# Decoder layer with latent attention: scores over 128 rows, regrouped query columns, and each mixer product's first weights loaded one product early

## The chip, the cores and the metric

One program on one core of a Trainium2 chip. The metric is the device time of one execution, in microseconds (us); three executions of the kernel before were timed, and one execution of it was profiled.

## What is computed

One decoder layer over 256 positions of width 2048, in float32. A SwiGLU feed-forward with 5632 hidden columns, a token mixer, and a second feed-forward, each followed by a residual layer norm. The token mixer runs two groups of heads on the same normalised stream: eight heads of latent attention, and eight heads of a sparse attention with three branches. The latent attention is this part:

```python
q = (rms_norm(c_q, q_norm_g) @ w_uq).reshape(b, s, MLA_HEADS, MLA_NOPE_DIM + MLA_ROPE_DIM)   # 512 -> 8 x (128 + 64)
q_nope, q_rope = q[..., :128], rope(q[..., 128:], pos)
kv = (rms_norm(c_kv, kv_norm_g) @ w_ukv).reshape(b, s, MLA_HEADS, 128 + 128)                 # 256 -> 8 x (k_nope, v)
k_r = rope(k_rope, pos)                                                                      # 64 wide, one for all heads
sc = (einsum("bhqd,bhkd->bhqk", qn, k_nope) + einsum("bhqd,bkd->bhqk", qr, k_r)) * scale     # causal, per block of 128 queries
o = einsum("bhqk,bhkd->bhqd", softmax(where(mask, sc, NEG_INF)), v)
```

c_q (512 wide), c_kv (256), k_rope (64), the sparse attention's projections and its gates are columns of one product of the stream with w_in.

## The kernel before

**Weight products.** Each product with a weight is done in three TensorE passes (`mm3`, L84 to L88): a float32 operand is split into a high part and the rest, high by high, high by low and low by high are added up in one PSUM bank, and all three run as 512-column matmuls of the fp32r type. The activations (`thi`, `tlo`) are the stationary operand, 128 x 128; the weights (`whi`, `wlo`) move, up to 512 columns. `load` (L133) brings 256 rows of one chunk of weight columns (512 KB for 512 columns) by one DMA of SP's queue into a buffer `raw` or `sum`; ACT casts it to `whi` (L81), and DVE subtracts to get `wlo` (L82). `whi` and `wlo` have six buffers each, `raw` and `sum` five and three.

`gemm` (L169) runs one chunk of columns over all of its rows, for the two tiles t of 128 positions: at each piece of 256 rows `load`, 6 matmuls for t = 0, 6 for t = 1, then two ticks. At the last piece `finish(0, ...)` is called between the two sixes and `finish(1, ...)` after them.

**Order of the work.** PE and SP carry out their instructions in the order in which the code issues them. Side work (transposes of results, scores, softmax, products with the values) is written as generators which `spawn` puts into lanes; `tick` counts and lets each lane issue its next step when it is due. A result's transposes come `DTR = 7` ticks after its `finish`. On ACT and DVE a scheduler orders the instructions, outside the program's text.

**The mixer.** The main sequence stands at L623 to L648 and L965 to L983: w_in chunk 0 (`fin_a`, c_q), `w_in_b` (`fin_b`, c_kv, rotated key, gates), w_in chunk 3 (`fin_c`), then for head group 0 `mla_proj(0)`, `mla_att(0)`, w_in chunks 4 and 1, `mla_proj(1)`, `mla_att(1)`, w_in chunks 5 and 2, and the output projection, with the sparse attention's side work between them.

`mla_proj(g)` (L703) does four heads by four products: two chunks of w_uq with 384 columns (two heads of 128 + 64), two of w_ukv with 512 columns. `fin_q` (L707) copies the 128-wide parts, rotates the 64-wide parts on DVE, and transposes each head's two parts apart: a 128-wide one (L718) and a 64-wide one (L719), 8 transposes for one chunk and both tiles. The rotated query parts and the rotated key `krT` (L589, L617) lie on 64 partitions.

`mla_att(g)` (L754) has three units: the second tile of queries for heads 0 and 1, then for heads 2 and 3, and the first tile for all four. For each head and each block of 128 keys there are two plain f32 matmuls into the same place, one over 128 rows and one over 64:

```python
o = ps[:, h * K + b * P:h * K + (b + 1) * P]
PE.matmul(o, qnT[t][:, hh, :], knT[b][:, hh, :], start=True, stop=False)   # L764, 128 rows
PE.matmul(o, qrT[t][:, hh, :], krT[:, b, :], start=False, stop=True)       # L765, 64 rows
```

That makes 8 instructions in each unit, 48 in the kernel. In the functions below, the line numbers are those of the profile.

Of the kernel before, what the change touches and what calls it, by code (L numbers as in the profile page):

```python
# [18 lines left out]
P = 128  # L19
D = 2048  # L20
# [24 lines left out]
def layer(ctx: ExitStack, tc: tile.TileContext, a: dict, out: bass.AP):  # L45
# [86 lines left out]

    def load(w, c, pc, spare=False):  # L133

        ap, pairs, n = w[:3]
# [33 lines left out]
    def gemm(x, w, c, ks, finish, head=0, tail=0, spare=0, first=KT, each=None):  # L169
# [419 lines left out]
    krT = att.tile([RD, NT, P], F32, name="krT")  # L589
# [12 lines left out]
    def fin_b(t, ps):  # L602
        def go():
            o = rms(ps[:, :KVR], KVR)
            kr = work.tile([P, 1, RD], F32, name="kr")
            rope(kr, ps[:, KVR:KVR + RD].rearrange("p (h d) -> p h d", h=1), cst["cos64"][:, t, :],
                 cst["sin64"][:, t, :], 1, RD)
            z = stat.tile([P, 24], F32, name="gz")
# [8 lines left out]
            PE.transpose(pt[:RD, 0, :], kr[:, 0, :], ident)  # L617
            A.copy(krT[:, t, :], pt[:RD, 0, :])
# [4 lines left out]
    gemm(xin, w_in, 0, KALL, fin_a, head=HEAD, spare=SPARE)  # L623
    gemm(xin, W["w_in_b"], 0, KALL, fin_b)
# [23 lines left out]
    gemm(xin, w_in, 3, KALL, fin_c)  # L648
# [51 lines left out]
    def units(t):  # L700
        return [(0, 4)] if t == 0 else [(0, 2), (2, 2)]

    def mla_proj(g):  # L703
        qnT, qrT, knT, vm = ([am() for _ in range(NT)] for _ in range(4))
        qrT = [q[:RD] for q in qrT]

        def fin_q(hp):  # L707
            def fin(t, ps):
                def go():
                    pv = ps.rearrange("p (h d) -> p h d", h=2)  # L710
                    qt = wk([P, 3, HD])
                    A.copy(qt[:, 0:2, :], pv[:, :, 0:HD])
                    rope(qt[:, 2, :].rearrange("p (h d) -> p h d", h=2), pv[:, :, HD:], cst["cos64"][:, t, :],
                         cst["sin64"][:, t, :], 2, RD)
                    yield DTR
                    pt = new_bank().rearrange("p (a b) -> p a b", a=4)
                    for j in range(2):
                        PE.transpose(pt[:, j, :], qt[:, j, :], ident)  # L718
                        PE.transpose(pt[:RD, 2 + j, :], qt[:, 2, j * RD:(j + 1) * RD], ident)  # L719
                    A.copy(qnT[t][:, 2 * hp:2 * hp + 2, :], pt[:, 0:2, :])  # L720
                    A.copy(qrT[t][:, 2 * hp:2 * hp + 2, :], pt[:RD, 2:4, :])
                    flag("mq", g, hp, t)

                spawn(go(), f"mla{g}q{hp}{t}")
                steps()
            return fin

        def fin_kv(hp):
            def fin(t, ps):
                def go():  # L730
# [8 lines left out]
                    A.copy(knT[t][:, 2 * hp:2 * hp + 2, :], pt[:, 0:2, :])  # L739
# [5 lines left out]

        for hp in range(2):
            h0 = 4 * g + 2 * hp
            gemm(lambda k, t: sl(cq[t], k), W["mla_w_uq"], h0 // 2, list(range(4)), fin_q(hp))
        for hp in range(2):
            h0 = 4 * g + 2 * hp  # L750
            gemm(lambda k, t: sl(ckv[t], k), W["mla_w_ukv"], h0 // 2, list(range(2)), fin_kv(hp))
        return g, qnT, qrT, knT, vm

    def mla_att(g, qnT, qrT, knT, vm):  # L754
        def unit(t, h0, nh):
            K = (t + 1) * P
            for hp in range(h0 // 2, (h0 + nh) // 2):
                yield from until(("mq", g, hp, t), *[("mk", g, hp, b) for b in range(t + 1)])
# [47 lines left out]
    def q_proj(g):  # L806
# [15 lines left out]
        gemm(xin, w_in, 1 + g, KALL, fin)  # L822
# [5 lines left out]
    def compress(src, n):  # L828
# [28 lines left out]
        hid = att.tile([P, 2, 32], F32, name="hid", bufs=2)  # L857
# [107 lines left out]
    mla_att(*mla_proj(0))  # L965
# [3 lines left out]
    gemm(xin, w_in, 4, KALL, fin_kv2("sel"), each=lambda i: ln_res("ln1", i // 2) if i % 2 else None)  # L969
    q_proj(0)  # L970
    mla_att(*mla_proj(1))
    new_kv("win")
    gemm(xin, w_in, 5, KALL, fin_kv2("win"))
    nsa_att(0)
    q_proj(1)
# [37 lines left out]
_CHUNKS = {"w_in": (D, NCH), "w_in_b": (D, 344), "mla_w_uq": (QR, 384), "mla_w_ukv": (KVR, NCH), "w_out": (D, NCH)}  # L1013
# [58 lines left out]
```

## Time and profile before

| | us |
|---|---|
| three timed runs | 1799.69, 1799.92, 1803.29 |
| their median | 1799.92 |
| the profiled execution, its own time | 1798.44 |
| its span, first to last instruction | 1796.7 |
| PE's matmul records, busy | 1772.0 |
| DVE, busy | 1500.6 |
| ACT, busy | 967.7 |
| the mixer's stretch of the span, about | 700 to 1070 |

How to read it: the profile shows for each engine when an instruction ran and, for a gap, what ended it. A matmul's record lasts longer than its turn on the engine (the next begins before it ends), so PE's busy time says only that PE was seldom empty; what a matmul costs is the time from its start to the next one's start. An f32 matmul is carried out in two passes and has two records; an fp32r one has one.

### The profile page before, as it was taken

Reading aid. Unit: us, or ns where it says so; the run is one execution under the profiler, and the core shown is the slowest. Engines: PE = TensorE matmul, PEld = TensorE weight load, DVE = VectorE, ACT = ScalarE, POOL = GpSimd, SP = SyncE. Lnnn points to the kernel's source line nnn. Section 1 sums busy time; section 2 is a strip of 40 time slices with the busy share of each in tenths; the row PEclk is TensorE's granted clock in tenths of the full one; section 3 lists DMA queues with packets and bytes.
Section 4 is the critical chain, followed back from the end, with each engine's and each line's share of the span. In section 5 each row is a group of like instructions: output and inputs, shape, how many; then the busy total and the mean of one; then the engine's idle time right before and its main releaser. Section 6 shows DMA issues by size and latency. Waiting matters only on the chain. (4 is left out here: it accounts for less than half of the span.)

```text
span 1796.7 us, 22556 instructions
## 1 busy us (share of the span) xinstructions
PE 1772.0 (99%) x8194; PEld 1453.9 (81%) x8194; DVE 1500.6 (84%) x1987; ACT 967.7 (54%) x1277; POOL 17.5 (1%) x40
## 2 busy tenths in 40 slices
PE   8999999999999999999999999999999999999997
PEld 6888888888888888887788787878888888888886
DVE  7899799999699976766566687899899999799976
ACT  6556455565456555644455555556456565456541
POOL 0000000000000000000000000000000000000000
PEclk9999999999999999999999999999999999999999
DMA  9656555557356575556733353567556557456673
GB/s 316 229 203 213 178 194 188 194 204 252 133 199 213 196 252 174 169 175 204 272 127 129 118 175 135 194 188 245 176 190 209 200 196 241 147 201 208 206 244 105
DMA packets 120736, 350.02 MB, mean 195 GB/s; under 512 B 11168, under 2 KB 17584, under 8 KB 120624
## 3 DMA queue, kind: packets, MB, share of 16 engines
q1 hardware_dynamic: 119312, 344.37, 56.0%
q0 software_dynamic: 1312, 4.21, 0.9%
q8 instruction: 64, 1.05, 0.2%
q14 instruction: 48, 0.39, 0.1%
HBM read 346.44 MB, written 2.10 MB: 194 GB/s over the span
## 5 line engine op out<-in xcount | busy, mean ns | idle before, releaser
L86 PE MATMUL bank<-whi,thi 128*128 128x512 f32 (+2 forms) x2046 | 805.5, 394 | 3.9 <-ACT whi L81 2.2
L87 PE MATMUL bank<-wlo,thi 128*128 128x512 f32 (+2 forms) x2046 | 793.7, 388 | 2.8 <-DVE wlo L82 2.8
L88 PE MATMUL bank<-whi,tlo 128*128 128x512 f32 (+2 forms) x2046 | 793.9, 388 | 0.2
L81 ACT CAST whi<-raw 128x1024 fp32r<-128x1024 f32 (+2 forms) x533 | 510.4, 975 | 409.2 <-PE bank L88 312.0
L82 DVE TENSOR_TENSOR wlo<-raw,whi 128x1024 fp32r<-128x1024 f32 (+2 forms) x533 | 590.0, 1123 | 101.8 <-ACT whi L81 99.3
L86 PEld LDWEIGHTS bank<-whi,thi 128*128 128x128 f32 x2046 | 384.3, 188 | 86.7 <-issue 5.4
L88 PEld LDWEIGHTS bank<-whi,tlo 128*128 128x128 f32 x2046 | 384.1, 188 | 80.3 <-DVE tlo L82 1.9
L87 PEld LDWEIGHTS bank<-wlo,thi 128*128 128x128 f32 x2046 | 384.6, 188 | 78.6 <-DVE wlo L82 5.0
L81 ACT CAST whi<-sum 128x1024 fp32r<-128x1024 f32 x265 | 274.6, 1047 | 288.4 <-PE bank L88 166.1
L82 DVE TENSOR_TENSOR wlo<-sum,whi 128x1024 fp32r<-128x1024 f32 x265 | 316.1, 1212 | 72.0 <-ACT whi L81 71.8
L243 DVE TENSOR_TENSOR sum<-raw 128x1024 f32<-128x1024 f32 x88 | 107.3, 1219 | 38.1 <-DMA raw<-in_ffn_w_gate 18.6
L87 PE MATMUL bank<-wlo,m 128*128 128x512 f32 x352 | 137.4, 390 | 0.2
L88 PE MATMUL bank<-whi,m 128*128 128x512 f32 x352 | 137.0, 389 | 0.0
L86 PE MATMUL bank<-whi,m 128*128 128x512 f32 x352 | 136.9, 389 | 0.0
L87 PEld LDWEIGHTS bank<-wlo,m 128*128 128x128 f32 x352 | 66.1, 188 | 15.2 <-DVE wlo L82 1.7
L86 PEld LDWEIGHTS bank<-whi,m 128*128 128x128 f32 x352 | 66.1, 188 | 13.9
L88 PEld LDWEIGHTS bank<-whi,m 128*128 128x128 f32 x352 | 66.1, 188 | 13.5
L275 DVE TENSOR_TENSOR w<-bank,w 128x512 f32<-128x512 f32 x96 | 62.6, 681 | 0.0
L245 DVE TENSOR_TENSOR sum<-sum,raw 128x512 f32<-128x512 f32 x88 | 60.2, 684 | 0.7
L244 DVE TENSOR_TENSOR sum<-sum,raw 128x512 f32<-128x512 f32 x88 | 60.1, 683 | 0.3
L82 DVE TENSOR_TENSOR tlo<-bank,thi 128x512 fp32r<-128x512 f32 (+1 forms) x56 | 35.8, 645 | 5.0 <-ACT thi L81 4.7
L660 ACT ACTIVATE w<-w,mx 128x256 f32<-128x256 f32 (+1 forms) x48 | 21.3, 446 | 29.2 <-DVE mx L656 29.2
(187 smaller groups left out, 890.2 us busy)
## 6 DMA issues: line engine op xcount, KB each, us to landing
raw<-in_ffn_w_up SPq DMA_DIRECT2D x160, 512.0 KB, 4.7
raw<-in_ffn_w_gate SPq DMA_DIRECT2D x148, 512.0 KB, 4.9
raw<-in_ffn_w_down SPq DMA_DIRECT2D x134, 512.0 KB, 4.7
sum<-in_ffn_w_down SPq DMA_DIRECT2D x42, 512.0 KB, 7.0
raw<-in_ffn_gu SPq DMA_DIRECT2D x32, 512.0 KB, 4.8
raw<-in_w_in SPq DMA_DIRECT2D x30, 512.0 KB, 4.7
raw<-in_w_out SPq DMA_DIRECT2D x20, 512.0 KB, 3.2
sum<-in_w_in SPq DMA_DIRECT2D x18, 512.0 KB, 6.7
```

The source lines that it names most:

```text
L81: A.copy(hi, src)
L82: V.tensor_tensor(lo, src, f(hi), op=OP.subtract)
L86: PE.matmul(ps, xh, wh, start=first, stop=False)
L87: PE.matmul(ps, xh, wl, start=False, stop=False)
L88: PE.matmul(ps, xl, wh, start=False, stop=last)
L243: V.tensor_tensor(t13, a_, b_[:, 1:2, :].broadcast_to([P, 2, NCH]), op=OP.add)
L244: V.tensor_tensor(t24[:, 0], t13[:, 0], a_[:, 1], op=OP.add)
L245: V.tensor_tensor(t24[:, 1], t24[:, 0], b_[:, 0], op=OP.add)
L275: V.tensor_tensor(r, B[b], r, op=OP.add)
L660: A.activation(s[:, h, :], s[:, h, :], AF.Exp, bias=mx[:, h:h + 1], accum_out=sm[:, h:h + 1])
```

## The change

1. The host regroups w_uq's columns: first the 128-wide parts of all eight heads, then the 64-wide parts of all eight; three chunks of 512 columns in place of four of 384. A new product of w_uq's third chunk gives all rotated query parts at once (`fin_qr`), ahead of `mla_proj(0)`; `mla_proj(g)` has one product of w_uq (four heads).
2. The rotated query parts are transposed by pairs of heads, 128 rows each. The rotated key is written twice into a zeroed tile, into the upper and the lower 64 of 128 columns, and transposed twice, so that `krT[:, j]` has the key on the rows of head j of a pair and zeros on the other 64.
3. A score matmul takes all keys of the unit at once: 256 columns for the second tile of queries, 128 for the first. `knT` is kept by pairs of heads with both key blocks side by side.
4. `gemm` gets `nxt`: before `finish(0, ...)` it loads (and splits) the first piece of the product that comes next, and that product takes it from `ahead`. All products from w_in chunk 0 to the last q_proj have it.
5. `hid` in `compress` has one buffer in place of two.

```diff
+    ahead = {}
     def load(w, c, pc, spare=False):
+        if (id(w), c, pc[0]) in ahead:
+            return ahead.pop((id(w), c, pc[0]))
...
             if end:
+                if nxt:
+                    ahead[id(nxt[0]), nxt[1], nxt[2]] = load(nxt[0], nxt[1], [nxt[2] + j for j in range(KT)])
                 finish(0, ps[0])
...
-    krT = att.tile([RD, NT, P], F32, name="krT")
+    krT = att.tile([P, 2, NT, P], F32, name="krT")
...
-            kr = work.tile([P, 1, RD], F32, name="kr")
-            rope(kr, ps[:, KVR:KVR + RD]...)
+            kr = wk([P, 2, P])
+            V.memset(kr, 0.0)
+            rope(kr[:, 0:1, :RD], ps[:, KVR:KVR + RD]...)
+            V.tensor_copy(kr[:, 1, RD:], kr[:, 0, :RD])
...
-            PE.transpose(pt[:RD, 0, :], kr[:, 0, :], ident)
-            A.copy(krT[:, t, :], pt[:RD, 0, :])
+            for j in range(2):
+                PE.transpose(pt[:, j, :], kr[:, j, :], ident)
+            A.copy(krT[:, :, t, :], pt[:, 0:2, :])
...
+    def fin_qr(t, ps):
+        def go():
+            qt = wk([P, NCH])
+            qv = qt.rearrange("p (h d) -> p h d", d=RD)
+            rope(qv, ps.rearrange("p (h d) -> p h d", d=RD), cst["cos64"][:, t, :], cst["sin64"][:, t, :], 8, RD)
+            yield DTR
+            pt = new_bank().rearrange("p (a b) -> p a b", a=4)
+            for j in range(4):
+                PE.transpose(pt[:, j, :], qt[:, j * P:(j + 1) * P], ident)
+            A.copy(qrT[t], pt)
+            flag("mr", t)
...
+        gemm(lambda k, t: sl(cq[t], k), uq, g, list(range(4)), fin_q, nxt=(ukv, 2 * g, 0))
         for hp in range(2):
-            gemm(lambda k, t: sl(cq[t], k), W["mla_w_uq"], h0 // 2, list(range(4)), fin_q(hp))
-        for hp in range(2):
-            gemm(lambda k, t: sl(ckv[t], k), W["mla_w_ukv"], h0 // 2, list(range(2)), fin_kv(hp))
+            gemm(lambda k, t: sl(ckv[t], k), ukv, 2 * g + hp, list(range(2)), fin_kv(hp),
+                 nxt=nxt if hp else (ukv, 2 * g + 1, 0))
...
-                for b in range(t + 1):
-                    o = ps[:, h * K + b * P:h * K + (b + 1) * P]
-                    PE.matmul(o, qnT[t][:, hh, :], knT[b][:, hh, :], start=True, stop=False)
-                    PE.matmul(o, qrT[t][:, hh, :], krT[:, b, :], start=False, stop=True)
+                o = ps[:, h * K:(h + 1) * K]
+                PE.matmul(o, qnT[t][:, hh, :], knT[hh // 2][:, hh % 2]...[:, :K], start=True, stop=False)
+                PE.matmul(o, qrT[t][:, 2 * g + hh // 2, :], krT[:, hh % 2]...[:, :K], start=False, stop=True)
...
-    mla_att(*mla_proj(0))
+    gemm(lambda k, t: sl(cq[t], k), uq, 2, list(range(4)), fin_qr, nxt=(uq, 0, 0))
+    mla_att(*mla_proj(0, (w_in, 4, 0)))
```

The order of the instructions at three places. In the rows, a number behind a name is a buffer's; x4 says that four equal instructions follow each other.

PE, the first unit of scores of head group 0, before (the last row is work of the compressed branch that follows):

```order
L764 MATMUL bank_7112<-m_6813,m_6810 128x128
L765 MATMUL bank_7112<-krT_6157,m_6812 128x128
L764 MATMUL bank_7112<-m_6814,m_6810 128x128
L765 MATMUL bank_7112<-krT_6157,m_6812 128x128
L764 MATMUL bank_7112<-m_6813,m_6810 128x128
L765 MATMUL bank_7112<-krT_6157,m_6812 128x128
L764 MATMUL bank_7112<-m_6814,m_6810 128x128
L765 MATMUL bank_7112<-krT_6157,m_6812 128x128
L847 MATMUL bank_7071<-raw_7133,w_7037 32x256 x4
```

Four pairs, each a 128-row and a 64-row operand. Now, the same unit:

```order
L783 MATMUL bank_7102<-m_6875,m_6874 128x256
L785 MATMUL bank_7102<-krT_6157,m_6822 128x256
L783 MATMUL bank_7102<-m_6875,m_6874 128x256
L785 MATMUL bank_7102<-krT_6157,m_6822 128x256
L868 MATMUL bank_7061<-raw_7119,w_7027 32x256 x4
L86 MATMUL bank_7001<-whi_7127,thi_6110 128x512
```

Eight instructions that changed between a 128-row and a 64-row operand became four; `krT` has taken part as a 128-row operand in each second one.

ACT, head group 1: L720 and L721 copy the transposed queries out of PSUM (after PE's transposes into bank_7854 and bank_7861), L81 casts weights. Before, PE's next matmul behind those transposes is the first that reads whi_7870:

```order
L852 COPY w_7850<-bank_7557 128x256
L720 COPY m_7600<-bank_7854 128x256
L721 COPY m_7602<-bank_7854 64x256
L720 COPY m_7601<-bank_7861 128x256
L721 COPY m_7603<-bank_7861 64x256
L81 CAST whi_7870<-raw_7868 128x1024
L81 CAST whi_7896<-raw_7894 128x1024
```

The cast of whi_7870 stands behind the copies of both banks. Now, where L743 copies the transposed queries (bank_7748, bank_7754), and PE's next matmul behind those transposes is the first that reads whi_7762:

```order
L81 CAST whi_7762<-sum_7760 128x1024
L837 COPY m_7685<-bank_7680 128x512
L837 COPY m_7692<-bank_7687 128x512
L754 COPY w_7708<-bank_7694 128x256
L755 COPY m_7592<-bank_7694 128x256
L81 CAST whi_7794<-sum_7792 128x1024
L754 COPY w_7717<-bank_7695 128x256
L755 COPY m_7593<-bank_7695 128x256
L743 COPY m_7588<-bank_7748 128x512
L743 COPY m_7589<-bank_7754 128x512
L81 CAST whi_7841<-raw_7839 128x1024
```

The cast that PE reads next stands eight rows ahead of the copies of the transposed queries; whi_7794, for the piece after it, stands ahead of them too.

DVE, second tile of `fin_b`: the rotation ends (L575 before, L582 now) and the transposed latent is scaled (L480 before, L487 now). Before:

```order
L575 TENSOR_TENSOR kr_6608<-kr_6608,w_6609 128x64
L82 TENSOR_TENSOR wlo_6760<-raw_6757,whi_6759 128x1024
L611 TENSOR_SCALAR gz_6614<-gz_6614 128x24
L612 RECIPROCAL gates_6158<-gz_6614 128x24
L82 TENSOR_TENSOR wlo_6778<-raw_6775,whi_6777 128x1024
L480 TENSOR_SCALAR w_6682<-bank_6679,pack_356 128x128 x2
L480 TENSOR_SCALAR w_6695<-bank_6692,pack_356 128x128 x2
```

Two splits of weights stand between the rotation and the scaling. Now:

```order
L582 TENSOR_TENSOR w_6616<-w_6616,w_6618 128x64
L487 TENSOR_SCALAR w_6686<-bank_6683,pack_356 128x128
L617 COPY w_6616<-w_6616 128x64
L487 TENSOR_SCALAR w_6686<-bank_6683,pack_356 128x128
L621 TENSOR_SCALAR gz_6624<-gz_6624 128x24
```

The copy of the key's second half (L617 of the changed kernel, w_6616) stands behind the first scaling of bank_6683. PE's transposes there now (L482 the latent, L628 the key):

```order
L482 MATMUL bank_6683<-ident_87,w_6585 128x128 x2
L628 MATMUL bank_6691<-ident_87,w_6587 128x128 x2
L482 MATMUL bank_6697<-ident_87,w_6614 128x128 x2
L628 MATMUL bank_6705<-ident_87,w_6616 128x128 x2
L86 MATMUL bank_6631<-whi_6711,thi_6110 128x512
```

The second of the transposes into bank_6705 reads what that copy writes, and the scaling ahead of the copy waits for PE's transposes into bank_6683, four to six places ahead of it.

## Rows read from the trace of the kernel before

**Rows 1.** The page of the profile: its first line, the busy time of each engine (us, share of the span, instructions), and the granted TensorE clock in 40 slices of the span, in tenths of full speed.
```profile
span 1796.7 us, 22556 instructions
...
PE 1772.0 (99%) x8194; PEld 1453.9 (81%) x8194; DVE 1500.6 (84%) x1987; ACT 967.7 (54%) x1277; POOL 17.5 (1%) x40
...
PEclk9999999999999999999999999999999999999999
```

**Rows 2.** The waits of PE from 700 to 1100 us, the stretch that holds the token mixer: instruction that waited <- what ended the wait: us in total, times, longest. The list is complete.
```profile
PE bank L86 <- ACT thi L81: 2.5, 3, 1.7
PE bank L86 <- ACT whi L81: 1.8, 1, 1.8
PE bank L87 <- DVE wlo L82: 0.8, 1, 0.8
PE bank L88 <- DVE tlo L82: 0.7, 2, 0.4
```

**Rows 3.** Groups of PE instructions with shapes kept apart: the two lines of the latent attention's scores. An f32 matmul leaves two records, one for each of its passes, so x48 is 24 instructions. Busy time in us and mean ns of one record.
```profile
L764 PE MATMUL bank<-m 128*128 128x128 f32 x48 | 11.1, 313 | 0.0
L765 PE MATMUL bank<-krT,m 64*128 64x128 f32 x48 | 11.6, 322 | 0.0
```

**Rows 4.** Timeline of PE, one unit of scores (second tile of queries, one pair of heads: 8 instructions, 16 records): start us, duration us, line, out<-in, partitions x columns, records. Durations overlap, so a price is read from one start to the next. The last row is the work that follows the unit.
```profile
810.90 0.38 PE L764 MATMUL bank<-m 128*128 128x128 f32 x2
811.21 0.49 PE L765 MATMUL bank<-krT,m 64*128 64x128 f32 x2
...
813.71 0.49 PE L765 MATMUL bank<-krT,m 64*128 64x128 f32 x2
814.12 0.64 PE L847 MATMUL bank<-raw,w 128*32 128x256 f32 x8
```

**Rows 5.** Timeline of PE at f32 products of other lines, same columns: values by probabilities in full rows (821.52), scores of the sparse attention with 256 columns in full rows (961.63), and a product over 15 rows (949.22), each with the row that follows it.
```profile
821.52 1.05 PE L770 MATMUL bank<-w,m 128*128 128x128 f32 x8
822.40 0.39 PE L764 MATMUL bank<-m 128*128 128x128 f32 x2
...
949.22 0.69 PE L918 MATMUL bank<-w,vcmp 15*128 15x256 f32 x2
949.84 1.13 PE L921 MATMUL bank<-w,m 128*128 128x256 f32 x4
...
961.63 1.03 PE L911 MATMUL bank<-m 128*128 128x256 f32 x4
962.50 1.03 PE L921 MATMUL bank<-w,m 128*128 128x256 f32 x4
```

**Rows 6.** Timeline of PE in the query projection: the first and the eighth matmul of a run of eight with 384 columns, the first and the twelfth of a run of twelve with 512 columns, and the first and the last of a block of eight transposes with the second matmul behind it.
```profile
782.73 0.33 PE L87 MATMUL bank<-wlo,thi 128*128 128x384 f32 x1
...
783.94 0.34 PE L88 MATMUL bank<-whi,tlo 128*128 128x384 f32 x1
...
787.11 0.39 PE L86 MATMUL bank<-whi,thi 128*128 128x512 f32 x1
...
789.64 0.39 PE L88 MATMUL bank<-whi,tlo 128*128 128x512 f32 x1
...
796.21 0.27 PE L718 MATMUL bank<-ident,w 128*128 128x128 f32 x1
...
796.97 0.27 PE L719 MATMUL bank<-ident,w 128*64 128x128 f32 x1
...
797.31 0.39 PE L87 MATMUL bank<-wlo,thi 128*128 128x512 f32 x1
```

**Rows 7.** Timeline of PE at the second block of query transposes of the second head group; in brackets the idle time before a row, and what ended it.
```profile
884.56 0.27 PE L718 MATMUL bank<-ident,w 128*128 128x128 f32 x1
...
887.36 0.50 PE L86 MATMUL bank<-whi,thi 128*128 128x512 f32 x1 [1.77 <-ACT whi L81]
888.62 0.50 PE L87 MATMUL bank<-wlo,thi 128*128 128x512 f32 x1 [0.76 <-DVE wlo L82]
888.96 0.40 PE L88 MATMUL bank<-whi,tlo 128*128 128x512 f32 x1
```

**Rows 8.** Timeline of ACT over the same time.
```profile
881.89 0.37 ACT L852 COPY w<-bank 128x256 f32<-128x256 f32 x1
885.19 0.37 ACT L720 COPY m<-bank 128x256 f32<-128x256 f32 x1 [2.93 <-PE bank L719]
...
886.25 3.90 ACT L81 CAST whi<-raw 128x1024 fp32r<-128x1024 f32 x4
```

**Rows 9.** Timelines of PE and of DVE where the transposes of the normalised latent and of the rotated key stand.
```profile
763.56 0.38 PE L475 MATMUL bank<-ident,w 128*128 128x128 f32 x2
...
764.10 0.27 PE L617 MATMUL bank<-ident,kr 128*64 128x128 f32 x1
...
761.15 0.22 DVE L575 TENSOR_TENSOR kr<-kr,w 128x64 f32<-128x64 f32 x1
...
763.98 1.12 DVE L480 TENSOR_SCALAR w<-bank,pack 128x128 f32<-128x128 f32 x4
```

**Rows 10.** Groups with shapes kept apart: the two halves of a weight's split into a high and a low part, on ACT and on DVE.
```profile
L82 DVE TENSOR_TENSOR wlo<-raw,whi 128x1024 fp32r<-128x1024 f32 x433 | 520.6, 1218 | 86.5 <-ACT whi L81 84.0 <-DMA raw<-in_ln_b 1.5
L81 ACT CAST whi<-raw 128x1024 fp32r<-128x1024 f32 x433 | 448.9, 1053 | 300.6 <-PE bank L88 227.9 <-DMA raw<-in_ffn_w_gate 18.9 <-issue 15.5
```

More of the change, by code (lines that the diff above doesn't have):

```diff
@@ L167, in new_bank, with gemm @@
         return bank.tile([P, NCH], F32, name="bank")
-    def gemm(x, w, c, ks, finish, head=0, tail=0, spare=0, first=KT, each=None):
+    def gemm(x, w, c, ks, finish, head=0, tail=0, spare=0, first=KT, each=None, nxt=None):
         n = w[2]
@@ L698, in layer @@
     NSC = float(HD ** -0.5)
[L700 to L726, printed above, removed]
@@ new lines, in layer @@
+    qrT = []
+    def fin_qr(t, ps):
[9 more added lines that the diff above has]
+            flag("mr", t)
+        spawn(go(), f"mlar{t}")
+        steps()
@@ new lines, in mla_proj, with fin_q, go @@
+    def mla_proj(g, nxt):
+        qnT, knT, vm = ([am() for _ in range(2)] for _ in range(3))
+        knT = [k.rearrange("p (h t) q -> p h t q", h=2) for k in knT]
+        def fin_q(t, ps):
+            def go():
+                qt = wk([P, 4, HD])
+                A.copy(qt, ps.rearrange("p (h d) -> p h d", h=4))
+                yield DTR
+                pt = new_bank().rearrange("p (a b) -> p a b", a=4)
+                for j in range(4):
+                    PE.transpose(pt[:, j, :], qt[:, j, :], ident)
+                A.copy(qnT[t], pt)
+                flag("mq", g, t)
+            spawn(go(), f"mla{g}q{t}")
+            steps()
@@ L744, in fin_kv, with mla_att @@
             return fin
+        gemm(lambda k, t: sl(cq[t], k), uq, g, list(range(4)), fin_q, nxt=(ukv, 2 * g, 0))
         for hp in range(2):
[L747 to L754 removed]
+            gemm(lambda k, t: sl(ckv[t], k), ukv, 2 * g + hp, list(range(2)), fin_kv(hp),
+                 nxt=nxt if hp else (ukv, 2 * g + 1, 0))
+        return g, qnT, knT, vm
+    def mla_att(g, qnT, knT, vm):
         def unit(t, h0, nh):
             K = (t + 1) * P
+            yield from until(("mr", t), ("mq", g, t))
             for hp in range(h0 // 2, (h0 + nh) // 2):
[L758 removed]
+                yield from until(*[("mk", g, hp, b) for b in range(t + 1)])
             ps = new_bank()
@@ L761, in unit @@
                 hh = h0 + h
-                for b in range(t + 1):
-                    o = ps[:, h * K + b * P:h * K + (b + 1) * P]
-                    PE.matmul(o, qnT[t][:, hh, :], knT[b][:, hh, :], start=True, stop=False)
-                    PE.matmul(o, qrT[t][:, hh, :], krT[:, b, :], start=False, stop=True)
+                o = ps[:, h * K:(h + 1) * K]
+                PE.matmul(o, qnT[t][:, hh, :], knT[hh // 2][:, hh % 2].rearrange("p t q -> p (t q)")[:, :K], start=True,
+                          stop=False)
+                PE.matmul(o, qrT[t][:, 2 * g + hh // 2, :], krT[:, hh % 2].rearrange("p t q -> p (t q)")[:, :K],
+                          start=False, stop=True)
             pT = yield from causal(ps[:, :nh * K], t, nh, MSC, None)
@@ L804, in layer, with q_proj @@
     qTs = {}
-    def q_proj(g):
+    def q_proj(g, nxt):
         def fin(t, ps):
@@ L856, in compress @@
             PE.transpose(pt[:, m, :], hs[:, m * P:(m + 1) * P], ident)
-        hid = att.tile([P, 2, 32], F32, name="hid", bufs=2)
+        hid = att.tile([P, 2, 32], F32, name="hid", bufs=1)
         x = stat.tile([P, 2, 32], F32, name="gx", bufs=2)
@@ L963, in out_last @@
             steps()
-    mla_att(*mla_proj(0))
+    qrT += [am() for _ in range(NT)]
+    gemm(lambda k, t: sl(cq[t], k), uq, 2, list(range(4)), fin_qr, nxt=(uq, 0, 0))
+    mla_att(*mla_proj(0, (w_in, 4, 0)))
     spawn(compress(kcT, "k"), "C")
@@ L968, in layer @@
     new_kv("sel")
-    gemm(xin, w_in, 4, KALL, fin_kv2("sel"), each=lambda i: ln_res("ln1", i // 2) if i % 2 else None)
-    q_proj(0)
-    mla_att(*mla_proj(1))
+    gemm(xin, w_in, 4, KALL, fin_kv2("sel"), each=lambda i: ln_res("ln1", i // 2) if i % 2 else None,
+         nxt=(w_in, 1, 0))
+    q_proj(0, (uq, 1, 0))
+    mla_att(*mla_proj(1, (w_in, 5, 0)))
     new_kv("win")
-    gemm(xin, w_in, 5, KALL, fin_kv2("win"))
+    gemm(xin, w_in, 5, KALL, fin_kv2("win"), nxt=(w_in, 2, 0))
     nsa_att(0)
-    q_proj(1)
+    q_proj(1, (W["w_out"], 0, 0))
     nsa_att(1)
```

17 lines of the change are left out of this document (10 added, 7 removed).

## The prediction

> **What bounds the kernel now.** I read the page first. PE is busy for 1772.0 of 1796.7 us, DVE for 1500.6, and the granted clock stands at its upper level, 2.4 GHz, in all 40 slices [rows 1]. So the time is the sum of PE's turns, and a change counts as far as it shortens that sum or removes a wait of PE; time saved on ACT, DVE or the queues is worth nothing by itself. The waits of PE come next: over the stretch that holds the mixer there are 2.5 + 1.8 + 0.8 + 0.7 = 5.8 us [rows 2]. That list sets the limit for the early loads: they can give back only a wait that PE has. Two of its four rows (thi, tlo) wait for activations behind a layer norm, which no early weight touches. The other two, 1.8 us for whi and 0.8 us for wlo, are one place, looked at below. Last I read the timeline of PE for what each kind of matmul costs from start to start, because the records overlap.
>
> **The scores.** A unit takes from 810.90 to 814.12, 3.22 us for 8 instructions, or 0.40 us each [rows 4]. There are 24 instructions on each of the two lines [rows 3], six units, together 6 x 3.22 = 19.3 us. This is dear for what it does: the product of the values, as wide and as many columns but in full rows only, does four f32 instructions (8 records) from 821.52 to 822.40, 0.22 us each [rows 5]. Where a 15-row product stands ahead of a full one, a 256-column instruction takes 949.84 - 949.22 = 0.62 us, while two full-row ones of that width take 962.50 - 961.63 = 0.87 us, 0.435 each [rows 5]. So 0.2 us is paid in both places at an instruction whose row count differs from its neighbour's. I read that as the price of changing rows.
>
> The change makes 32 instructions, all over 128 rows: in four units 4 of 256 columns each (16), in two units 8 of 128 (16), as the order of PE shows. At full-row prices that is 16 x 0.435 + 16 x 0.22 = 7.0 + 3.5 = 10.5 us, a gain of 8.8 us. No row shows a 128-row instruction with krT, so I bound it. The dear end is that the price has nothing to do with rows and stays: 16 x 0.40 + 16 x 0.62 = 6.4 + 9.9 = 16.3 us, a gain of 3.0. The cheap end is 8.8 itself, as no f32 row of these widths is cheaper. I take 8.8: in rows 5 the cheap prices belong to accumulating pairs as well as to single products, and what the scores have alone is the change of rows.
>
> The Trainium skill speaks against this: the page "TensorE: Matmul & The Clock Gate", section "Part 3: Packing small matmuls — row/col tiling", says that a weight load overlaps a running matmul only when its row group differs. By that rule full rows behind full rows would never overlap, and the sum would take the dear end, 16.3 us. The rows with eight full-row records at 0.11 us each disagree with it.
>
> **The projections.** Seven steps with 384 columns take 783.94 - 782.73 = 1.21 us, 0.173 each; eleven with 512 take 789.64 - 787.11 = 2.53 us, 0.230 each [rows 6]. Four chunks of 24 matmuls become three: 96 x 0.173 = 16.6 against 72 x 0.230 = 16.6 us. I put it at nothing. The bytes are the same, 3 MB.
>
> **The transposes.** Seven steps in a block take 796.97 - 796.21 = 0.76 us, 0.109 each, whether they write 128 or 64 rows [rows 6]. The queries have 24 in place of 32, the key 4 in place of 2: six fewer, a gain of 0.65 us.
>
> **The wait that goes.** In head group 1, PE begins a block of eight query transposes at 884.56, and the second matmul behind it starts at 888.62, 4.06 us later; at the same place in head group 0 that takes 797.31 - 796.21 = 1.10 us [rows 6, 7]. With the 0.34 us to the third matmul in place of 0.23, the place costs 3.1 us, more than the 2.6 us of rows 2 since the records overlap. Its cause stands in ACT's timeline: ACT has nothing to do from 882.26 to 885.19, held by a copy (L720) that needs those transposes, and only after four copies does it turn to the casts, the first at 886.25 [rows 8]. They are in ACT's queue behind the copies. In the new order that cast stands eight rows ahead of the copies, and the next piece's too, so I take the whole 3.1 us as a gain. What is late next there is the value of the piece after it, whi_7841: it stands behind the copies, but PE reads it only after two units of 12 matmuls and a unit of scores, some 7 us.
>
> **The new wait.** The key's second half is copied on DVE behind the first scaling of the latent, which waits for PE. Before, PE's transposes began at 763.56 and DVE's scaling at 763.98 [rows 9]. From there 0.28 us for one scaling (four take 1.12) and 0.22 us for a copy of that size, as L575's row has it [rows 9], give 764.48; PE would reach the transpose that reads it at 763.56 + 7 x 0.109 = 764.32. So it waits some 0.2 us, with what a semaphore takes 0.3 us. Bounds: nothing, where DVE is early, and 1.5 us, where a split of 1.22 us [rows 10] comes between. The memsets and copies besides run on DVE, which has 296 us to spare.
>
> **The early loads elsewhere.** Each of the other boundaries shows no wait of PE [rows 2], so they give nothing. What they add is order: the same DMA, cast and split, moved ahead of `finish`. On SP a load moves ahead of the loads of the compressed branch; on ACT 1.05 us and on DVE 1.22 us [rows 10] can come to stand ahead of a result's copies. The cover is the seven ticks until its transposes, two ticks being a piece of 12 matmuls, so about 7 x 6 x 0.23 = 9.7 us [rows 6]. I put them at nothing. `hid` in one buffer costs nothing: both branches stand in one lane, and the second writes it only after its own eight loads and products.
>
> **The sum.** 8.8 + 0 + 0.65 + 3.1 - 0.3 = 12.3 us (rounded). The profiled execution took 1798.44 us, so 1786.2 us against that execution; the median of the runs, 1799.92, lies 1.5 us above it, and I forecast for a median: 1787.6 us.
>
> **The rivals.** (1) *The rows are not what is dear.* Only the number of score instructions falls, and the sum takes 16.3 us for them: 5.8 us less gain, 1793.4 us. For it speaks that no row shows this very pair in full rows; against it, that two pairs of rows, at 128 and at 256 columns, agree on the 0.2 us [rows 4, 5]. Chance 0.10. It is what the Trainium skill's rule named above would give. (2) *The wait moves.* ACT's and DVE's order is the scheduler's, and one cast behind a held copy somewhere else in the mixer costs what this one did: 3.1 us are not gained, 1790.7 us. Against it: at no place that I read in the order does PE's next weight stand behind copies of its last transposes. Chance 0.10. (3) *Slower: the early split stands in front of the results.* At 14 boundaries a cast and a split, 1.05 + 1.22 = 2.27 us, would come ahead of the copies that PE's transposes need; if PE waited for all of it, 14 x 2.27 = 31.8 us, so 1787.6 + 31.8 = 1819.4 us. It decides once the copies have less than 2.3 us in hand, and it must do so at six or more of the boundaries to eat the gain; the seven ticks give about 9.7 us. Chance 0.04. (4) *Hidden anyway.* The scores overlap with something that I take as serial, and the sum comes out within 3.6 us of before, 1797 us or so. Against it: while a unit of scores runs, no other matmul starts on PE [rows 4]. Chance 0.04.
>
> **How the numbers follow.** The forecast has 0.72. About 0.2%, 3.6 us, is what a measurement of this kernel can tell from no change. The forecast and rivals 1 and 2 lie more than that below the median: 0.92 for faster. Rival 4 is 0.04 for the same, rival 3 is 0.04 for slower. The range: down to 1783.5, if the runs agree with the profiled execution (1.5 us) and the key's wait and some starts of blocks come out better; up to 1793.5, which takes in rivals 1 and 2.
>
> **What would show it.** In the new profile the second-tile score units take about 1.7 us and those of the first tile 1.8, on the two score lines x32 and x32 records, with no 0.4 us step at 128 columns. PE's waits in the mixer have no row of 1.8 us for whi at the second head group's query transposes, and a new one of some tenths at the key's transposes. The blocks of query transposes are three. It is wrong if the steps from one score line to the other stay at 0.4 us, if a wait for whi or for a copied result of over 1 us appears behind one of the boundaries, or if the time is above 1793.5.

## The result and the profile after

The changed kernel takes 1784.87 us (median of 4 runs, 1784.16 to 1785.57), the kernel before beside it 1800.68 (4 runs, 1799.69 to 1803.29): ratio 0.991, 95% interval 0.9893 to 0.9927. Run again with the last set of experiments it took 1787.64 (5 runs, 1786.08 to 1788.19) against 1800.13 (9 runs, 1797.29 to 1803.48): 0.993, interval 0.9917 to 0.9944. The forecast, 1787.6 (range 1783.5 to 1793.5), stands between the two medians. The profiled execution took 1784.83 us against 1798.44.

The page, as [rows 1]: PE is 11.0 us less busy, and the granted clock shows 9 tenths or more in all slices.

```profile
PE 1761.0 (99%) x8132; PEld 1445.5 (81%) x8132; DVE 1499.9 (84%) x1965; ACT 965.1 (54%) x1261; POOL 17.5 (1%) x40
...
PEclk9999999999999999999999999999999999999999
```

PE's waits from 700 to 1100 us, the answer to [rows 2]. Those for whi and wlo are gone; one of 0.5 us at the key's transposes (L628) is new.

```profile
PE bank L86 <- ACT thi L81: 2.5, 3, 1.7
PE bank L88 <- DVE tlo L82: 0.7, 2, 0.4
PE bank L628 <- DVE w L582: 0.5, 1, 0.5
```

Timeline of PE at the scores, as [rows 4]: a unit of the second tile (four instructions of 256 columns), then a part of a unit of the first tile (eight of 128). Columns as there.

```profile
807.52 0.60 PE L783 MATMUL bank<-m 128*128 128x256 f32 x2
807.95 0.59 PE L785 MATMUL bank<-krT,m 128*128 128x256 f32 x2
...
809.34 0.64 PE L868 MATMUL bank<-raw,w 128*32 128x256 f32 x8
...
822.85 0.39 PE L783 MATMUL bank<-m 128*128 128x128 f32 x2
823.07 0.39 PE L785 MATMUL bank<-krT,m 128*128 128x128 f32 x2
```

The steps are 0.43 and 0.22 us, where [rows 4] has 0.40 at 128 columns: the full-row prices of [rows 5], at a pair of instructions that no row of before showed. At the second head group's query transposes, where PE stood in [rows 7], it no longer stops: from the start of the eight transposes to the first matmul behind them it takes 879.74 - 878.89 = 0.85 us, where [rows 7] has 887.36 - 884.56 = 2.80. ACT has cast the weight that PE reads next (871.70) well ahead of the copies of the transposed queries (PE, then ACT):

```profile
878.89 1.09 PE L742 MATMUL bank<-ident,w 128*128 128x128 f32 x8
879.74 0.48 PE L86 MATMUL bank<-whi,thi 128*128 128x512 f32 x1
```

```profile
871.70 1.05 ACT L81 CAST whi<-sum 128x1024 fp32r<-128x1024 f32 x1 [0.49 <-DMA sum<-in_w_in]
...
879.59 1.07 ACT L743 COPY m<-bank 128x512 f32<-128x512 f32 x2 [3.70 <-PE bank L742]
```

**A finer measure than the runs.** In every kernel here the first transposes of the normalised latent (763.56 in [rows 9]) and the matmul that waits for thi behind the second layer norm bound the part of the mixer that was changed (the first two of the 14 early loads lie ahead of it). The two rows of the changed kernel:

```profile
763.14 0.38 PE L482 MATMUL bank<-ident,w 128*128 128x128 f32 x2
...
1085.83 0.50 PE L86 MATMUL bank<-whi,thi 128*128 128x512 f32 x1 [1.74 <-ACT thi L81]
```

and the later one of the kernel before:

```profile
1098.47 0.50 PE L86 MATMUL bank<-whi,thi 128*128 128x512 f32 x1 [1.74 <-ACT thi L81]
```

From the one to the other take 334.91 us before and 322.69 after: 12.22 us less. The same two rows of each further profile:

| kernel | from, to (us) | stretch | runs, median |
|---|---|---|---|
| before | 763.56, 1098.47 | 334.91 | 1800.68 |
| before, profiled again | 762.96, 1097.86 | 334.90 | 1797.75 (1 run) |
| before + early loads | 764.62, 1099.47 | 334.85 | 1799.51 |
| before + pack load on POOL | 763.83, 1095.66 | 331.83 | 1794.55 |
| before + copies on VectorE | 762.77, 1096.87 | 334.10 | 1796.88 (1 run) |
| full rows alone | 762.53, 1090.59 | 328.06 | 1792.31 |
| full rows + pack load on POOL | 763.05, 1086.52 | 323.47 | 1786.48 |
| change without early loads | 763.68, 1086.44 | 322.76 | 1785.38 |
| change | 763.14, 1085.83 | 322.69 | 1784.87 |
| change, again | 763.03, 1085.74 | 322.71 | 1787.64 |
| change, rotated products over 64 rows | 763.21, 1091.69 | 328.48 | 1790.56 |
| change, both products over 64 rows | 762.97, 1087.54 | 324.57 | 1787.04 |
| change, key's rotation first | 763.25, 1085.19 | 321.94 | 1783.82 |

The same kernel profiled twice agrees within 0.02 us, so this stretch tells tenths apart where the medians of the change moved by 2.8 us from one set of runs to another. The kernel before beside the runs: 1800.68 for the change, 1799.36 in the first set of experiments, 1800.22 in the second, 1800.13 in the third.

### The profile page after: what moved, and what is told of

The parts are those of the page before. It is cut to its first block, busy times and chain, and to the rows that moved or that the text cites. A ratio compares the mean times of both kernels' runs of the same rounds, so it can differ in the third digit from the quotient of the medians.

```text
span 1783.1 us, 22369 instructions
## 1 busy us (share of the span) xinstructions
PE 1761.0 (99%) x8132; PEld 1445.5 (81%) x8132; DVE 1499.9 (84%) x1965; ACT 965.1 (54%) x1261; POOL 17.5 (1%) x40
## 5 line engine op out<-in xcount | busy, mean ns | idle before, releaser
L86 PE MATMUL bank<-whi,thi 128*128 128x512 f32 (+1 forms) x2038 | 804.0, 394 | 2.2 <-ACT thi L81 1.7
L87 PE MATMUL bank<-wlo,thi 128*128 128x512 f32 (+1 forms) x2038 | 792.3, 389 | 1.9 <-DVE wlo L82 1.9
L88 PE MATMUL bank<-whi,tlo 128*128 128x512 f32 (+1 forms) x2038 | 792.5, 389 | 0.1
L81 ACT CAST whi<-raw 128x1024 fp32r<-128x1024 f32 (+2 forms) x534 | 513.0, 977 | 412.4 <-PE bank L88 316.5
L81 ACT CAST whi<-sum 128x1024 fp32r<-128x1024 f32 x262 | 271.7, 1048 | 279.9 <-PE bank L88 162.7
L250 DVE TENSOR_TENSOR sum<-raw 128x1024 f32<-128x1024 f32 x88 | 107.6, 1223 | 28.9 <-DMA raw<-in_ffn_w_gate 16.1
```

Of the source, the lines that this page charges most:

```text
L81: A.copy(hi, src)
L86: PE.matmul(ps, xh, wh, start=first, stop=False)
L87: PE.matmul(ps, xh, wl, start=False, stop=False)
L88: PE.matmul(ps, xl, wh, start=False, stop=last)
L250: V.tensor_tensor(t13, a_, b_[:, 1:2, :].broadcast_to([P, 2, NCH]), op=OP.add)
```

## The experiments

**1. Full rows alone.** To the kernel before only this is done, with the key's two halves of the change and `hid` in one buffer:

```diff
-                        PE.transpose(pt[:, j, :], qt[:, j, :], ident)
-                        PE.transpose(pt[:RD, 2 + j, :], qt[:, 2, j * RD:(j + 1) * RD], ident)
+                    for j in range(3):
+                        PE.transpose(pt[:, j, :], qt[:, j, :], ident)
...
-                    PE.matmul(o, qrT[t][:, hh, :], krT[:, b, :], start=False, stop=True)
+                    PE.matmul(o, qrT[t][:, hh // 2, :], krT[:, hh % 2, b, :], start=False, stop=True)
```

> The kernel before with one part of the change alone: the rotated parts stand in 128 rows (head pairs, the key in two halves with zeros beside them), but the scores stay cut by key block, 48 instructions of 128 columns, with no merged columns, no regrouped query product and no early loads. Theory (what is dear is the change of row count from one instruction to the next): every score instruction takes 0.22 us from start to start, the six units 48 x 0.22 = 10.6 us in place of 19.3, a gain of 8.7; the query transposes are 24 in place of 32 and the key's 4 in place of 2 (0.65 us), the key's wait of 0.7 us comes, and the wait of 3.1 us for whi at the second head group's query transposes stays. So about 8.7 us below the kernel before on the same chip, ratio 0.995. Rival (the number of instructions is what is dear): the units stay at 0.40 us an instruction, 19.3 us, and the time stays within 1 us of before.

Measured: 1792.31 us (1790.73 to 1793.34) against 1799.36, ratio 0.9959, interval 0.9947 to 0.9972. The score steps are 0.22 us with 48 instructions still, so the count is not what is dear:

```profile
809.36 0.38 PE L765 MATMUL bank<-m 128*128 128x128 f32 x2
809.58 0.39 PE L766 MATMUL bank<-krT,m 128*128 128x128 f32 x2
```

The gain of the runs, 7.05 us, is short of 8.7; in the stretch it is 334.91 - 328.06 = 6.85. The trace says why. Timeline of PE behind the wait for whi, and the windows over it (columns of the second: window, its length, busy us and instructions of PE, PEld, DVE, ACT and POOL, granted clock, DMA share, GB/s):

```profile
882.46 0.50 PE L86 MATMUL bank<-whi,thi 128*128 128x512 f32 x1 [1.69 <-ACT whi L81]
883.72 0.50 PE L87 MATMUL bank<-wlo,thi 128*128 128x512 f32 x1 [0.76 <-DVE wlo L82]
...
884.74 0.62 PE L88 MATMUL bank<-whi,tlo 128*128 128x512 f32 x1
...
887.72 0.81 PE L739 MATMUL bank<-ident,w 128*128 128x128 f32 x4
888.28 0.48 PE L86 MATMUL bank<-whi,thi 128*128 128x512 f32 x1
```

```profile
884.00:886.00 2.00, 2.00 (x7) 1.57 (x7) 2.00 (x3) 1.25 (x2) 0.00 (x0) 0.68 1.02 414
886.00:888.00 2.00, 2.00 (x7) 1.50 (x6) 1.07 (x1) 0.00 (x0) 0.00 (x0) 0.50 1.02 399
```

After two waits of 1.69 and 0.76 us the granted clock fell to half, 1.2 GHz (0.68 is the mean of a stretch in which it fell, 0.50 a stretch wholly at the lower level). Seven steps take 887.72 - 884.74 = 2.98 us, 0.43 each in place of 0.23, which is 1.4 us lost, and the four transposes take 0.56 in place of 4 x 0.109 = 0.44: 1.5 us together. Without them the gain is 8.35 us.

**2. The change with 64 rows.** In the changed kernel, the rotated product reads `qrT[t][:RD, ...]` and `krT[:RD, 0]`:

> The changed kernel with the rotated products of the scores over 64 rows in place of 128 (it leaves out the odd heads' rotated parts and takes the even heads' in their place), all else the same: 32 score instructions with merged columns. Theory (a change of rows costs 0.2 us at each instruction): 16 instructions of 256 columns at 0.62 and 16 of 128 at 0.40 make 16.3 us in place of 10.5, so 5.8 us more than the changed kernel, about 1790.7 us. Rival (the merged columns gave the gain, rows cost nothing): steps of 0.43 and 0.22 us and a time within 1 us of the changed kernel.

Measured: 1790.56 us (1790.12 to 1790.58), and 328.48 - 322.69 = 5.79 us in the stretch, where 5.8 was expected. Its PE at the second-tile unit:

```profile
808.11 0.70 PE L785 MATMUL bank<-krT,m 64*128 64x256 f32 x2
808.73 0.70 PE L783 MATMUL bank<-m 128*128 128x256 f32 x2
...
809.99 0.64 PE L868 MATMUL bank<-raw,w 128*32 128x256 f32 x8
```

0.62 to 0.63 us a step. Merged columns without full rows leave the scores at 16.1 us, summed from start to start, where rival 1 put 16.3; that rival's premise, that rows are not what is dear, falls with it.

**3. Both products over 64 rows.** The first product too reads `[:RD]` of both operands.

> The changed kernel with both products of the scores over 64 rows (it leaves out the other 64 rows of each product). Theory (it is the change of rows between neighbours, not few rows, that costs): inside a unit the steps are again 0.43 us at 256 columns and 0.22 at 128; only a unit's first instruction and the first one behind it change rows, at most 6 x 2 x 0.2 = 2.4 us, so 0 to 2.4 us above the changed kernel. Rival (64 rows are dear by themselves): 0.62 and 0.40 us at every one of the 32 instructions, the first products too, 5.8 us or more above the changed kernel.

Measured: 1787.04 us (1785.74 to 1791.63); in the stretch 1.88 us above the change. The unit:

```profile
806.87 0.60 PE L759 MATMUL bank<-ident,w 128*128 128x128 f32 x4
807.40 0.70 PE L783 MATMUL bank<-m 64*128 64x256 f32 x2
807.93 0.59 PE L785 MATMUL bank<-krT,m 64*128 64x256 f32 x2
808.36 0.59 PE L783 MATMUL bank<-m 64*128 64x256 f32 x2
```

Inside the unit the steps are 0.43, as in full rows; in the units of 128 columns they are 0.22 (823.66 to 823.88). Where transposes over 128 rows give way to 64, they take 0.53 in place of 0.44 and the first score 0.53 in place of 0.43. So few rows cost nothing, and a change of rows costs 0.2 us. That settles the term of 8.8 us. The runs spread over 5.9 us here; in the profiled one, 1788.87 us, the granted clock fell behind the stretch (experiment 9).

**4. The change without the early loads.** The two lines of `gemm` that fill `ahead` are taken out.

> The changed kernel without the early loads: each product loads its first weights when it begins, as before. Theory (the early loads gave nothing, and the regrouping of the query products took the wait of 3.1 us away, since in this order too the casts of the next product's first two weights stand ahead of the second head group's query copies on ScalarE): within 1 us of the changed kernel and no wait for whi in the mixer. Rival (the early loads took the wait away): a wait for whi of about 2 us at the second head group's query transposes, 3.1 us above the changed kernel.

Measured: 1785.38 us (1784.73 to 1787.39), stretch +0.07 us, no wait for whi.

**5. Before with the early loads alone.** `load`, `gemm` and the `nxt` arguments of the change, on the query chunks of before.

> The kernel before with the early loads alone, at the same 14 kinds of boundaries, its four query chunks of 384 columns included. Theory (the early loads give nothing by themselves; the wait at the second head group's query transposes comes from the weights that SP issues late, behind the compressed branch's load from the pack, which waits 10 us for a work buffer, and from the casts' place behind the copies on ScalarE, and neither changes here): PE's wait of 1.7 us for whi and 0.8 us for wlo stays, and the time stays within 1.5 us of the kernel before on the same chip. Rival (an early cast is what removes the wait): no such wait, 3.1 us below.

Measured: 1799.51 us (11 runs), ratio 1.0001, interval 0.9992 to 1.001; waits of 1.8 and 0.8 us for whi and wlo at the old place; stretch -0.06 us. So the early loads are worth nothing that the runs or the stretch show, with the change and without it.

**6. The pack load on another queue.** In the kernel before, SP's own waits from 860 to 892 us begin with this row (columns as in PE's waits):

```profile
SPq L851 <- PE bank L719: 10.0, 1, 10.0
```

L851 is the compressed branch's load of its second weights into a work buffer; it waits 10 us until the first block of query transposes frees one, and the weights of the next product stand behind it on SP, issued from 878.46 on. One line of before is changed:

```diff
-        nc.sync.dma_start(w2.rearrange("p m d -> p (m d)"), cst["w2_" + n])
+        G.dma_start(w2.rearrange("p m d -> p (m d)"), cst["w2_" + n])
```

> The kernel before with one line changed: the compressed branch's load of its second weights from the pack goes through POOL's queue, so that SP's weight loads no longer stand behind it. Nothing else is edited (the order that the scheduler then makes puts the cast of the next product's weight ahead of the copies on ScalarE too). Theory (the pack load that holds SP is the root of the wait): the waits for whi and wlo at the second head group's query transposes go, 3.1 us below the kernel before, and up to 1.8 us more where that wait had let TensorE's clock fall, as it did in the profile of the version with full rows alone (nine steps of 0.43 in place of 0.23 us). Rival (only the number and place of the query copies matters): the wait stays and the time is within 1 us of before.

Measured: 1794.55 us (1793.77 to 1796.14) against 1800.22, ratio 0.9971, interval 0.9959 to 0.9982; in the stretch 334.91 - 331.83 = 3.08 us. PE's waits in the mixer are now those for thi (2.5) and tlo (0.7) alone, and ACT casts ahead of the last four copies:

```profile
884.90 1.05 ACT L81 CAST whi<-raw 128x1024 fp32r<-128x1024 f32 x1 [1.74 <-DMA raw<-in_w_in]
...
887.17 0.37 ACT L720 COPY m<-bank 128x256 f32<-128x256 f32 x1
```

The medians fell by 5.7 us, the profiled executions by 3.66. The 2.6 us above 3.08 aren't placed: a fall of the clock behind the wait, as in experiment 1, is one candidate, but three profiles that have the wait (before twice, and experiment 5) show none at that place.

**7. Which queue held the cast.** In before, the last four copies of the second head group go to VectorE: `copy = V.tensor_copy if (g, hp) == (1, 1) else A.copy`.

> The kernel before with the second head group's last four query copies on VectorE in place of ScalarE, so that nothing holds ScalarE ahead of the cast of the next weight; SP's loads stay late. If ScalarE's queue alone held the cast, it starts where ScalarE falls idle, at 882.3 us of the trace of before; if the late load alone held it, it starts no sooner than before, at about 886.2; between the two, both did, and the start is the landing of a weight that is issued at 878.5 (4 to 5 us later, about 883). The four copies now stand ahead of the subtraction on VectorE, so PE still waits for wlo, some 2 us, and the time stays within 2 us of before.

Measured: 1796.88 us in one run, 0.81 us less in the stretch. ACT there:

```profile
881.10 0.37 ACT L853 COPY w<-bank 128x256 f32<-128x256 f32 x1
881.37 1.05 ACT L81 CAST whi<-raw 128x1024 fp32r<-128x1024 f32 x1
```

The cast starts as soon as ACT is free, where [rows 8] has it 4.4 us behind the same copy (881.89 to 886.25). The weight had landed, 3.6 us behind its issue at 877.67, and not 4 to 5 as I had put it. So ScalarE's order alone held the cast, as the prediction read it; the late load on SP is what that order follows, since moving the load alone turned it round (experiment 6). PE waited 2.0 us for wlo behind the copies on VectorE, as expected. The time was to stay within 2 us of before; it lies 3.3 us below the median beside it and 1.6 below the profiled execution of before, and one run can't settle it.

**8. The key's rotation first.** In the change, `fin_b` is written with memset, rotation and copy ahead of `rms`:

```diff
-            o = rms(ps[:, :KVR], KVR)
             kr = wk([P, 2, P])
...
             V.tensor_copy(kr[:, 1, RD:], kr[:, 0, :RD])
+            o = rms(ps[:, :KVR], KVR)
```

> The changed kernel with the key's rotation (memset, four products and sums, copy) written ahead of the latent's scaling. Theory (the wait of 0.5 us, a step of 0.91 in place of 0.22 us, comes from the second tile's rotation that stands late in VectorE's order, behind the scaling and a split of 1.16 us): the second pair of key transposes follows the first at 0.22 us again and the time falls by 0.7 us, too little to be told apart by the runs. Rival (it is the added copy in itself): the wait stays at half a microsecond or moves to the scaling, and PE waits for the latent's transposes.

In the changed kernel PE and DVE stand so at the second tile's key:

```profile
763.58 0.38 PE L482 MATMUL bank<-ident,w 128*128 128x128 f32 x2
764.49 0.69 PE L628 MATMUL bank<-ident,w 128*128 128x128 f32 x2 [0.53 <-DVE w L582]
764.93 0.48 PE L86 MATMUL bank<-whi,thi 128*128 128x512 f32 x1
```

```profile
762.69 1.16 DVE L82 TENSOR_TENSOR wlo<-raw,whi 128x1024 fp32r<-128x1024 f32 x1
...
764.21 0.22 DVE L582 TENSOR_TENSOR w<-w 128x64 f32<-128x64 f32 x1
764.35 0.34 DVE L487 TENSOR_SCALAR w<-bank,pack 128x128 f32<-128x128 f32 x1
764.61 0.18 DVE L617 COPY w<-w 128x64 f32<-128x64 f32 x1
```

and with the rotation first PE stands so:

```profile
763.69 0.38 PE L482 MATMUL bank<-ident,w 128*128 128x128 f32 x2
763.90 0.38 PE L628 MATMUL bank<-ident,w 128*128 128x128 f32 x2
764.04 0.48 PE L86 MATMUL bank<-whi,thi 128*128 128x512 f32 x1
```

The wait is gone, and the step is 0.21 us. The place gains more than that step: from the second tile's latent to the next weight matmul it takes 764.04 - 763.69 = 0.35 us in place of 764.93 - 763.58 = 1.35. The other 0.3 us are a second wait in the changed kernel, too short for the list of waits: the second transpose of the key reads what the copy (L617) writes, which ends at 764.79 behind the first scaling (L487), and it starts at 764.85, 0.36 us after the first in place of 0.11. The stretch is 0.75 us shorter, so a quarter of a microsecond came back elsewhere. 1783.82 us (4 runs, 1783.31 to 1784.64), ratio 0.9909, interval 0.9893 to 0.9924: the lowest median here, though by less than the two medians of the change differ.

**9. The two causes together, and both kernels again.** Experiments 1 and 6 in one kernel, against both kernels on one chip:

> The kernel before with two parts: the rotated parts in 128 rows (48 score instructions of 128 columns, as in the version with full rows alone) and the pack load on POOL's queue. No merged columns, no regrouped query product, no early loads. Theory (full rows and the wait are all that the change gave): scores at 0.22 us, no wait for whi, the key's wait of 0.7 us as in the changed kernel, so within 1.5 us of the changed kernel on the same chip. Rival (merged columns, the regrouped product or the early loads gave a part): over 2 us above the changed kernel.

Measured: 1786.48 us (1785.37 to 1786.81), 1.2 us below the change beside it, with a stretch of 323.47, 0.78 above it. So the runs show nothing beyond these two causes, and the stretch leaves 0.8 us for the rest. The change beside it:

> The changed kernel once more, beside the others: some 15 us below the kernel before (ratio 0.991 to 0.992), with runs that lie within 2 us of each other, where those of before spread over 5 us. If the spread of before comes from falls of TensorE's clock behind its waits, the changed kernel, which has one wait of over 1 us less, keeps the smaller spread; if it comes from the chip, both spread alike.

Measured: 1787.64 us, spread 2.1 us over 5 runs where under 2 was expected, against 6.2 over 9 runs for before. A smaller spread again, over fewer runs; that falls of the clock make it is not shown by this. Nor does the next run show it:

> The kernel before once more, for a second profile of one execution. Theory (the wait for whi lets the clock fall in some executions): if the time is 1 us or more above 1798.4, a stretch of the mixer or of the place behind the last layer norm runs at 1.2 GHz, each such stretch worth 1.5 to 1.9 us; if the time is about 1798, none does. Rival (the spread lies elsewhere): a longer execution without such a stretch.

Measured: 1797.75 us, the old waits and 334.90 us in the stretch. The granted clock stays at its upper level until PE has done its last matmul (1785.3 us) and falls behind it, where it costs PE nothing. It tells that the stretch repeats, and nothing of the longer executions.

Two profiles at hand tell something of those. In experiments 3 and 5 the clock fell right behind the wait of 1.74 us for thi that ends the stretch, a wait that every kernel here has: the mean granted clock is 0.59 from 1088 to 1090 us in the one and 0.55 from 1100 to 1102 us in the other. The first twelve steps behind that wait take 4.80 and 4.75 us there, 3.2 in the changed kernel and in before, and the span behind the stretch is 699.6 and 699.4 us long, 697.1 to 698.6 in the other eleven profiles. So such a fall makes some executions 1.5 us longer, and it can come behind a wait that the change leaves in place (experiment 3 is a version of the changed kernel). How much of the spread of before it explains stays open.

## Why the prediction was right, step by step

The sum was 12.3 us; the stretch gives 12.22. The two large terms, scores and wait, held in size and cause. That the sums meet within 0.1 us is partly luck: the scores gave 0.3 us more than was put down and the projections 0.5 more, and the new wait cost 0.7 more, which nearly cancels. Taken apart by pairs of kernels (the third also puts the pack load back on SP):

| part | from, to | us |
|---|---|---|
| full rows, with transposes and the key's wait | 331.83, 323.47 | 8.36 |
| the wait for whi and wlo | 334.91, 331.83 | 3.08 |
| merged columns and regrouped query product | 323.47, 322.76 | 0.71 |
| early loads | 322.76, 322.69 | 0.07 |

- **Scores, 8.8.** Right in size and cause: 0.22 and 0.43 us steps in the change, and experiments 1 to 3 show that it is the change of rows that costs. Summed from each score instruction's start to the next start on PE, the scores take 19.4 us in before, 10.7 in full rows with 48 instructions (experiment 9) and 10.3 in the change: 8.6 us for the rows, 0.4 for the merged columns.
- **The Trainium skill's rule against it.** The weight loads (PEld) of the changed kernel and of before, at the scores:

```profile
822.96 0.30 PEld L785 LDWEIGHTS bank<-krT,m 128*128 128x128 f32 x2
```

```profile
811.21 0.29 PEld L765 LDWEIGHTS bank<-krT,m 64*128 64x128 f32 x2
```

In full rows the load starts 0.11 us ahead of its matmul (823.07 above), under the running one; where rows change, it starts with its own matmul (811.21 in [rows 4]). The Trainium skill, page "TensorE: Matmul & The Clock Gate", section "Part 3: Packing small matmuls — row/col tiling", has a load overlap only when the row group differs. For these f32 products the trace disagrees: the load overlaps where the rows stay, and stops doing so where they change.

- **Transposes, 0.65.** Right: the query transposes take 4.9 us before and 4.1 in the change, 0.8 less, and two more of the key at 0.11 us take 0.2 of that back. With the scores (8.6) and the key's place (1.0, below) that makes the 8.36 of the table but for 0.1.
- **Projections, 0.** Mis-sized: summed in the same way, the 96 matmuls of 384 columns take 17.6 us (experiment 9) and the 72 of 512 that replace them 17.1 (experiment 4), a gain of 0.5 us. The steps of [rows 6] are those inside a run, 0.173 and 0.230; with the starts of the runs the means are 0.184 and 0.237. With the merged columns that is some 1.0 us, of which 0.3 are lost again at the transposes and the products with the values; the rest is the 0.71 of the table.
- **The wait that goes, 3.1.** Right to 0.02 us. The cast behind the copies was read rightly (experiment 7), but not why it stood there: the pack load on SP. The prediction left open whether the early loads or the regrouping took it away; it was the regrouping (experiment 4), as full rows alone and the early loads alone left the wait in place (experiments 1 and 5). In its order SP issues the loads of the two weights that PE reads next ahead of the pack load (872.23 in experiment 4, 871.71 in the change, 878.08 in before).
- **The new wait, 0.3.** Here the step failed in size: it measures 1.0 us. The copy on DVE behind the first scaling was read rightly and costs the forecast 0.3 (the second transpose waits for it, experiment 8). What was left out stands ahead of it: PE first waits for the rotation itself, which had come to stand behind a split of 1.16 us. The step to the key's transposes is 764.49 - 763.58 = 0.91 us in place of 0.22, so 0.69 more. Both together lie within the bounds (0 to 1.5), whose upper end named just such a split.
- **Early loads elsewhere, 0.** Right: 0.06 and 0.07 us. Rivals 2 and 3 did not come about.
- **From the sum to the median, +1.5.** The profiled execution gained 13.61 us: 12.22 in the stretch, 0.42 ahead of it and 0.97 behind it. These two are differences between executions: the two profiles of before differ by 0.60 ahead of the stretch, the two of the change by 1.3 behind it. The 1.5 us by which the median of before lay above its profile did not carry over to the first runs of the change (median 1784.87, profile 1784.83) and did to the second (1787.64, profile 1786.08). This step added a difference between executions as if it were a term; it is the range's business.

## What to carry to other kernels

Price a small matmul from start to start and look at the row counts of its neighbours: padding 64 rows with zeros to 128 saved 8.6 us of scores, because every change of rows cost 0.2 us. What it costs stands on another engine: the copy and the later rotation of the padded key on DVE made PE wait 1.0 us, and writing them earlier removed that wait. When a queue's order seems to cause a wait, look one queue further up for what made that order: here a 128 KB load that waited for a work buffer on SP cost 3.1 us two engines away, and one line moved it. Measure a small change between two rows of the trace that bound it, where medians can't tell it.

## What the runs showed of the hardware

- In a pair of f32 matmuls each costs 0.22 us at 128 columns and 0.43 at 256, over 64 rows as over 128, when neighbours agree in rows (experiments 1 and 3), and 0.40 to 0.42 and 0.62 to 0.63 when they alternate ([rows 4], experiment 2). Each leaves two records, 0.11 us apart at 128 columns; the text ahead of the prediction calls them passes, but how often the engine goes through the operands for one record no run here shows.
- Behind two waits of 1.69 and 0.76 us the granted clock fell to 1.2 GHz from 884.7 to about 888.1 (experiment 1), which cost 1.5 us besides the wait; behind the same waits it did not fall in three other profiles. Behind the wait of 1.74 us for thi it fell in two of 13 profiles (experiments 3 and 5), again for some 1.5 us.
